# A hybrid decoder layer on one core: TensorE's order from the output projection on, the first feed-forward block's partial sums and the norm's row sums rearranged

## The chip, the core and the metric

The kernel runs on one core of a Trainium2 chip. The metric is the device time of one execution in microseconds (us). A core has five engines with an instruction stream each: TensorE (PE; its weight loads are shown apart, as PEld), VectorE (DVE), ScalarE (ACT), GpSimd (POOL) and SyncE (SP, which here only issues transfers). Each works through its own stream in order; they wait for each other by semaphores. Matmul results are collected in PSUM banks, which VectorE and ScalarE read.

## What is computed

One layer with batch 1, 512 tokens, width 1024, in float32. Two attention branches run side by side, are gated and merged, and a SwiGLU feed-forward part follows:

```python
u = rms_norm(x, norm_mix_g)
proj = u @ w_in
...
merged = sigmoid(gate_sb) * y_sb + sigmoid(gate_dl) * y_dl
x = x + merged @ w_out
u2 = rms_norm(x, norm_ffn_g)
g_ff, up_ff = split(u2 @ w_ffn_in, 2)          # each 512 x 2816
x = x + (silu(g_ff) * up_ff) @ w_ffn_out
return rms_norm(x, norm_final_g)

def rms_norm(x, g):
    return x * rsqrt(mean(x * x, -1) + 1e-6) * g
```

## The kernel before, in words

**Layout.** Everything is kept feature-major: 128 features on the partitions, 512 tokens along the row, so that x is eight tiles of 128x512. Weights stand still in TensorE, activations move through it. Every float32 product is made of three matmuls in fp32r, on numbers split into a high part (a cast) and a low part (what the cast left over): high·high, high·low, low·high. For weights, ScalarE makes the high part (`whi`, L147) and VectorE the low part (`wlo`, L148). `next_weights()` hands out the next chunk of weights and splits two chunks ahead; the raw chunks are loaded by SyncE into a few rotating buffers.

**Stages.** Norm and input projection, the two attentions, the up-projections with their gates (they leave the merged activations as eight pairs mh, ml: the high and low parts of the eight feature tiles), the output projection, the feed-forward part, the last norm.

**Output projection** (before: from L770). It makes its eight feature tiles f in the order of HALVES = 0, 4, 1, 5, 2, 6, 3, 7. Each is 24 matmuls of 128x512 (8 values of k, three each) into a bank `po`; there are two such banks, so the third projection takes over the first one's. VectorE adds the bank to x (`res`, L774). Then come the operands of the feed-forward part: `forms_upper` for f < 4, `forms_lower` for f >= 4, which needs the matching upper one, and ScalarE squares x for the norm, which VectorE sums up in `acc`.

**Feed-forward block 0, 1, 2, ...** (`hidden(i)`). The kernel does the 22 blocks of the first feed-forward product with seven products in place of eight, in the manner of Strassen and Winograd. The seven operands are called B11, U1, B21, B22, T3, V2, T4. They are the seven quarters of 256 columns of `fh` (high parts) and `fl` (low parts), one such tile for each of four values of k; the last three (T3, V2, T4) are computed from both halves of x (`forml`, L763 to L765), cast on ScalarE (`fh`, L174) and their low part is made on VectorE (`fl`, L175, 128x768). The last value of k, 3, is ready last, as it needs the last projection f = 7. Of weights a block has four chunks: unit 0 (for B11 and B21), unit 1 (V2 and T3), unit 2 (U1 and T4) and unit 3 (B22). Units 1 and 2 share one load, `rawu`: VectorE adds its two loaded thirds into a third one (L136), unit 2 is split from it, and unit 1 from its sum with unit 0's raw chunk (`s`, L138). There are two buffers of rawu: that of block 2 can be loaded when block 0's unit 2 has been split into whi and wlo.

The sums are collected in two PSUM banks, `pf` (halves pa and p6) and `pg` (halves psum and pr). `times(ps, unit, half, form, ks)` issues three 128x256 matmuls for each k (L816, L817, L818 before the change). Some sums must be read in between: ScalarE copies q1, yv (from pa), q7 (from pr) and wv (L824). In block 0 the norm's factors are not known yet, so block 0 is finished later and the norm is put on the results.

**Norm.** `row_sums()` issues four small matmuls (L283, `ss`) on acc; VectorE scales the sums (L287), GpSimd raises them to the power -1/2 (`r`, L291). `row_spread()` spreads r over the partitions (`rb`, L298), in block 1, ahead of which nothing needs it.

**Order.** Each engine's order is chosen by a scheduler from the order of the program, with priorities (`tc.high_priority()`). Within `tc.manual_schedule(engines={PE})` TensorE's order is that of the program. Before, that began at the feed-forward loop (L966); the order of the other engines is the scheduler's throughout.

Of the kernel before, what the change touches and what calls it, by code (L numbers as in the profile page):

```python
# [16 lines left out]
P = 128  # L17
S = 512
D = 1024
KD = D // P  # L20
# [9 lines left out]
HALVES = [0, 4, 1, 5, 2, 6, 3, 7]  # L30
# [14 lines left out]
def trunk_kernel(ctx, tc, xT, gains, w_in, w_up, w_o, w_f, w_d, bias, out):  # L45
# [20 lines left out]
    def bank(tag, name):  # L66
        if tag == "proj":
            return pp.tile([P, S], F32, tag=tag, name=name, bufs=BANKS[tag])
        if ppool[1] is not None:
            return ppool[1].tile([P, S], F32, tag="att" if tag == "alpha" else "sums", name=name, bufs=BANKS["att"])  # L70
        return pair(name)[:, 0, :]
# [286 lines left out]
    def next_weights(ahead=2):  # L358
        w = weights(ci[0], ahead)
        ci[0] += 1  # L360
        return w

    def product(ps, mh_, ml_, w, nk, first=True, last=True, k0=0, between={}):
        hi, lo = w
        for k in range(nk):
            cs = slice(k * P, (k + 1) * P)
            mm3(ps, hi[:, cs], lo[:, cs], mh_[k0 + k], ml_[k0 + k], first and k == 0, last and k == nk - 1)
            tick()
            if k in between:
                with tc.high_priority():  # L370
                    between[k]()
# [385 lines left out]
    def forms_lower(j):  # L757
# [8 lines left out]
        V.scalar_tensor_tensor(out=lo[:, 2:4, :], in0=halves(x), scalar=g, in1=hi[:, 2:4, :].bitcast(F32), op0=ALU.mult, op1=ALU.subtract)  # L766
        split_to(hi[:, 4:, :], lo[:, 4:, :], raw)

    for f in HALVES:
        x = res(f)  # L770
        ps = bank("proj", f"po{f}")
        product(ps, mhi, mlo, next_weights(), KD)
        with tc.high_priority():
            V.tensor_tensor(out=x, in0=ps, in1=x, op=ALU.add)  # L774
        with tc.high_priority():
            if f >= 4:
                forms_lower(f - 4)
            else:
                forms_upper(f)
        norm_square(f, x, acc2, "2")  # L780

    def row_sums():
        ps = bank("att", "ss2")
        for j in range(4):
            row_sum(ps, acc2, j)
        rows["r2"] = row_factors(ps, 4, "2")
# [16 lines left out]
    def hidden(i):  # L803
# [7 lines left out]
        def times(ps, unit, half, form, ks=range(4), first=False, last=False):  # L811
            hi, lo = w[unit]
            for k in ks:
                cs = slice(half * S + k * P, half * S + (k + 1) * P)
                xhi, xlo = fh[k][:, form, :], fl[k][:, form, :]
                T.matmul(ps, hi[:, cs], xhi, start=first and k == 0, stop=False, skip_group_check=True)  # L816
                T.matmul(ps, hi[:, cs], xlo, start=False, stop=False, skip_group_check=True)  # L817
                T.matmul(ps, lo[:, cs], xhi, start=False, stop=last and k == 3, skip_group_check=True)  # L818

        def kept(ps, name):  # L820

            t = lsq[:, :hs] if name == "q1" and i == 0 else fp.tile([P, hs], F32, tag=f"kept{name}", name=f"{name}{i}")
            with tc.high_priority():
                A.copy(t, ps)  # L824
            return t
# [6 lines left out]
        if i == 0:  # L832

            w[1] = next_weights()
            times(pa, 0, 0, B11, first=True)
            q1 = kept(pa, "q1")
            times(psum, 0, 1, B21, range(3), first=True)
            w[2] = next_weights()
            times(pa, 2, 0, U1)
            yv = kept(pa, "yv")  # L840
            times(pr, 1, 1, T3, range(3))
            times(p6, 1, 0, V2, range(3))
            times(psum, 0, 1, B21, [3], last=True)
            times(pr, 1, 1, T3, [3])
            q7 = kept(pr, "q7")
            times(p6, 1, 0, V2, [3])
            wv = kept(p6, "wv")
            V.tensor_tensor(out=yv, in0=yv, in1=wv, op=ALU.add)
            w[3] = next_weights()
            times(pr, 2, 1, T4, last=True)  # L850
            times(pa, 3, 0, B22, last=True)
            V.tensor_tensor(out=g[:, hs:], in0=pa, in1=wv, op=ALU.add)
            V.tensor_tensor(out=wv, in0=wv, in1=q1, op=ALU.add)
        else:
            times(pa, 0, 0, B11, first=True)
            q1 = kept(pa, "q1")
            times(psum, 0, 1, B21, first=True, last=True)
            w[1] = next_weights()
            times(pa, 1, 0, V2)
            wv = kept(pa, "wv")  # L860
            times(pr, 1, 1, T3)
            q7 = kept(pr, "q7")
            if i == 1:
                row_sums()
            if i == 4:
                row_inverse()
            w[2] = next_weights()
            times(pa, 2, 0, U1)
            yv = kept(pa, "yv")
            times(pr, 2, 1, T4, last=True)  # L870
            if i == 1:
                row_spread()
                yield
            w[3] = next_weights()
            times(pa, 3, 0, B22, last=True)
# [87 lines left out]
            T.matmul(pw, warm, warm.unsqueeze(1).to_broadcast([P, 4, P]), start=True, stop=True)  # L963

    waiting = []
    order = tc.manual_schedule(engines={mybir.EngineType.PE})  # L966
    order.__enter__()
    for step in FFN:
        if step[0] == "in":
            waiting.append(hidden(step[1]))  # L970
# [100 lines left out]
```

## Time and profile before

| | us |
|---|---|
| median of 3 runs | 750.01 (749.42 to 750.14) |
| the profiled execution | 750.42 |
| its span (first to last instruction) | 748.7 |
| TensorE busy | 739.3 (99%) |
| VectorE busy | 530.0 (71%) |
| ScalarE busy | 365.8 (49%) |
| GpSimd busy | 80.4 (11%) |

The profile shows one execution. The mean granted TensorE clock is 0.997 of full speed. Rows below give start and duration in us, then engine, line, operation and tiles (out<-in); a bracket gives the time that the engine stood idle before the instruction, and what ended it.

### The profile page before, as it was taken

What the parts mean: (1) busy time and instruction counts of PE and PEld (TensorE: products, weight loads), DVE (VectorE), ACT (ScalarE), POOL (GpSimd) and SP (SyncE); (2) the same over time, 40 slices, a digit from 0 to 9 for tenths busy, and PEclk for the clock granted to TensorE, in tenths of its full rate; (3) what the DMA queues carried; (4) which work ended last, traced back from release to release, by engine and by line L of the source; (5) the groups of instructions that cost most, each with busy time, mean ns of one, the idle gap of its engine ahead of it and who ended that gap; (6) DMA issues with size and microseconds to landing.
All of it is one profiled execution on the core that took longest, in us unless ns stands there. A gap on an engine that the chain in (4) does not pass through costs nothing. (4 is left out here: it accounts for less than half of the span.)

```text
span 748.7 us, 10944 instructions
## 1 busy us (share of the span) xinstructions
PE 739.3 (99%) x4447; PEld 644.6 (86%) x4447; DVE 530.0 (71%) x685; ACT 365.8 (49%) x526; POOL 80.4 (11%) x48
## 2 busy tenths in 40 slices
PE   9999999999999999999999999999999999999996
PEld 6877777889888888888889999999999999999985
DVE  6446676576768883376997899778787777776643
ACT  7255756752423632332654666545445454444453
POOL 1005042250241030000001000000000000000033
PEclk9999999999999999999999999999999999999998
DMA  8322112122342232234313223233332333332223
GB/s 281 113 61 96 69 57 85 57 85 84 114 167 78 94 113 77 78 115 153 113 56 99 100 78 114 92 105 105 108 109 84 104 106 108 104 104 66 57 57 114
DMA packets 25187, 74.13 MB, mean 99 GB/s; under 512 B 2864, under 2 KB 5936, under 8 KB 25008
## 3 DMA queue, kind: packets, MB, share of 16 engines
q1 hardware_dynamic: 23664, 69.74, 28.8%
q0 software_dynamic: 784, 3.15, 1.2%
q8 instruction: 35, 0.57, 0.3%
q10 hardware_dynamic: 688, 0.54, 0.2%
q14 instruction: 16, 0.13, 0.1%
HBM read 71.32 MB, written 2.10 MB: 98 GB/s over the span
## 5 line engine op out<-in xcount | busy, mean ns | idle before, releaser
L147 ACT CAST whi<-raw 128x1024 fp32r<-128x1024 f32 (+2 forms) x114 | 108.7, 955 | 146.1 <-PE pg L817 33.9
L148 DVE TENSOR_TENSOR wlo<-raw,whi 128x1024 fp32r<-128x1024 f32 (+2 forms) x114 | 145.9, 1281 | 40.9 <-ACT whi L147 39.9
L816 PE MATMUL pf<-fh,whi 128*128 128x256 f32 x348 | 98.7, 284 | 0.1
L818 PE MATMUL pf<-fh,wlo 128*128 128x256 f32 x348 | 98.6, 283 | 0.0
L817 PE MATMUL pf<-fl,whi 128*128 128x256 f32 x348 | 98.5, 283 | 0.0
L816 PE MATMUL pg<-fh,whi 128*128 128x256 f32 x264 | 75.2, 285 | 0.6 <-ACT q L824 0.6
L817 PE MATMUL pg<-fl,whi 128*128 128x256 f32 x264 | 74.7, 283 | 0.0
L818 PE MATMUL pg<-fh,wlo 128*128 128x256 f32 x264 | 74.7, 283 | 0.0
L816 PEld LDWEIGHTS pf<-fh,whi 128*128 128x128 f32 x348 | 66.7, 192 | 0.9 <-ACT lsq L824 0.3
L817 PEld LDWEIGHTS pf<-fl,whi 128*128 128x128 f32 x348 | 66.7, 192 | 0.6
L818 PEld LDWEIGHTS pf<-fh,wlo 128*128 128x128 f32 x348 | 66.7, 192 | 0.3 <-DVE wlo L148 0.2
L147 ACT CAST whi<-s 128x1024 fp32r<-128x1024 f32 (+1 forms) x43 | 36.2, 842 | 33.8 <-PE pg L817 21.5
L148 DVE TENSOR_TENSOR wlo<-s,whi 128x1024 fp32r<-128x1024 f32 (+1 forms) x43 | 41.2, 959 | 14.9 <-ACT whi L147 14.7
L816 PEld LDWEIGHTS pg<-fh,whi 128*128 128x128 f32 x264 | 50.6, 192 | 1.3 <-ACT q L824 1.0
L817 PEld LDWEIGHTS pg<-fl,whi 128*128 128x128 f32 x264 | 50.6, 192 | 0.0
L818 PEld LDWEIGHTS pg<-fh,wlo 128*128 128x128 f32 x264 | 50.6, 192 | 0.0
L163 PE MATMUL pd<-hh,whi 128*128 128x512 f32 (+1 forms) x132 | 50.4, 382 | 0.0
L163 PE MATMUL pd<-hl,whi 128*128 128x512 f32 (+1 forms) x132 | 50.3, 381 | 0.0
L163 PE MATMUL pd<-hh,wlo 128*128 128x512 f32 (+1 forms) x132 | 50.1, 379 | 0.0
L920 POOL TENSOR_TENSOR inv<-inv,sq 128x256 f32<-128x256 f32 (+1 forms) x10 | 9.6, 963 | 317.4 <-ACT sq L919 315.3
L914 DVE TENSOR_TENSOR res<-pd,res 128x512 f32<-128x512 f32 (+1 forms) x36 | 22.6, 629 | 20.9 <-PE pd L163 20.7
L147 ACT CAST whi<-rawu 128x1024 fp32r<-128x1024 f32 x22 | 23.1, 1051 | 29.0 <-PE pd L163 23.5
(464 smaller groups left out, 1788.2 us busy)
## 6 DMA issues: line engine op xcount, KB each, us to landing
raw<-in_w_in_dram SPq DMA_DIRECT2D x43, 512.0 KB, 3.3
rawu<-in_w_ffn_in_dram SPq DMA_DIRECT2D x22, 512.0 KB, 3.2
raw<-in_w_ffn_in_dram SPq DMA_DIRECT2D x22, 512.0 KB, 3.4
raw<-in_w_ffn_out_dram SPq DMA_DIRECT2D x24, 384.0 KB, 3.1
raw<-in_w_out_dram SPq DMA_DIRECT2D x8, 512.0 KB, 3.3
raw<-in_w_up_dram SPq DMA_DIRECT2D x8, 384.0 KB, 3.0
x<-in_xT_dram SPq DMA_DIRECT2D x8, 256.0 KB, 4.2
res<-in_xT_dram POOLq DMA_DIRECT2D x8, 256.0 KB, 4.2
```

The source lines that it names most:

```text
L147: state["last"] = A.copy(hi[:, cs], r[:, cs])
L148: V.tensor_tensor(out=lo[:, cs], in0=r[:, cs], in1=hi[:, cs].bitcast(F32), op=ALU.subtract)
L163: return T.matmul(ps, a, b, start=start, stop=stop, skip_group_check=not check)
L816: T.matmul(ps, hi[:, cs], xhi, start=first and k == 0, stop=False, skip_group_check=True)
L817: T.matmul(ps, hi[:, cs], xlo, start=False, stop=False, skip_group_check=True)
L818: T.matmul(ps, lo[:, cs], xhi, start=False, stop=last and k == 3, skip_group_check=True)
L914: newest[1] = V.tensor_tensor(out=x, in0=ps, in1=x, op=ALU.add)
L920: G.tensor_tensor(out=rows["inv"][:, cs], in0=rows["inv"][:, cs], in1=sq[:, cs], op=ALU.add)
```

## The change

The output projection is issued by a new `out_part(f, ks)`, which can issue some values of k alone. TensorE's order is fixed by the program from there on: seven of the eight k of f=0, two of f=4, the last of f=0, the rest of f=4, and then one projection after the other. In block 0 the first three k of T3 and V2 are issued ahead of U1, and at its end the last k of T3 (with the copy q7) ahead of that of B21. The row sums are called at the end of block 0 instead of in block 1. Lines of the blocks move down by 15: L774 becomes L789, L816 to L818 become L831 to L833, L824 becomes L839.

```diff
--- before.py
+++ after.py
@@ -766,10 +766,25 @@
         V.scalar_tensor_tensor(out=lo[:, 2:4, :], in0=halves(x), scalar=g, in1=hi[:, 2:4, :].bitcast(F32), op0=ALU.mult, op1=ALU.subtract)
         split_to(hi[:, 4:, :], lo[:, 4:, :], raw)
 
+
+    begun = {}
+
+    def out_part(f, ks):
+        if f not in begun:
+            begun[f] = bank("proj", f"po{f}"), next_weights()
+        ps, (whi, wlo) = begun[f]
+        for k in ks:
+            cs = slice(k * P, (k + 1) * P)
+            mm3(ps, whi[:, cs], wlo[:, cs], mhi[k], mlo[k], k == 0, k == KD - 1)
+
+    order = tc.manual_schedule(engines={mybir.EngineType.PE})
+    order.__enter__()
+    out_part(HALVES[0], range(KD - 1))
+    out_part(HALVES[1], range(2))
     for f in HALVES:
         x = res(f)
-        ps = bank("proj", f"po{f}")
-        product(ps, mhi, mlo, next_weights(), KD)
+        out_part(f, [KD - 1] if f == HALVES[0] else range(2 if f == HALVES[1] else 0, KD))
+        ps = begun[f][0]
         with tc.high_priority():
             V.tensor_tensor(out=x, in0=ps, in1=x, op=ALU.add)
         with tc.high_priority():
@@ -835,20 +850,21 @@
             times(pa, 0, 0, B11, first=True)
             q1 = kept(pa, "q1")
             times(psum, 0, 1, B21, range(3), first=True)
+            times(pr, 1, 1, T3, range(3))
+            times(p6, 1, 0, V2, range(3))
             w[2] = next_weights()
             times(pa, 2, 0, U1)
             yv = kept(pa, "yv")
-            times(pr, 1, 1, T3, range(3))
-            times(p6, 1, 0, V2, range(3))
-            times(psum, 0, 1, B21, [3], last=True)
             times(pr, 1, 1, T3, [3])
             q7 = kept(pr, "q7")
+            times(psum, 0, 1, B21, [3], last=True)
             times(p6, 1, 0, V2, [3])
             wv = kept(p6, "wv")
             V.tensor_tensor(out=yv, in0=yv, in1=wv, op=ALU.add)
             w[3] = next_weights()
             times(pr, 2, 1, T4, last=True)
             times(pa, 3, 0, B22, last=True)
+            row_sums()
             V.tensor_tensor(out=g[:, hs:], in0=pa, in1=wv, op=ALU.add)
             V.tensor_tensor(out=wv, in0=wv, in1=q1, op=ALU.add)
         else:
@@ -860,8 +876,6 @@
             wv = kept(pa, "wv")
             times(pr, 1, 1, T3)
             q7 = kept(pr, "q7")
-            if i == 1:
-                row_sums()
             if i == 4:
                 row_inverse()
             w[2] = next_weights()
@@ -963,8 +977,6 @@
             T.matmul(pw, warm, warm.unsqueeze(1).to_broadcast([P, 4, P]), start=True, stop=True)
 
     waiting = []
-    order = tc.manual_schedule(engines={mybir.EngineType.PE})
-    order.__enter__()
     for step in FFN:
         if step[0] == "in":
             waiting.append(hidden(step[1]))
```

TensorE, at the end of the first two projections, before (po0 and po4 are the banks of f=0 and f=4, po1 that of the third projection, f=1; mh7 and ml7 are the last pair of merged activations):

```order
L163 MATMUL po4_2704<-mh5_2579,wlo55_2620 128x512
L163 MATMUL po0_2664<-mh7_2647,whi54_2585 128x512
L163 MATMUL po4_2704<-mh6_2613,whi55_2619 128x512
L163 MATMUL po4_2704<-ml6_2614,whi55_2619 128x512
L163 MATMUL po4_2704<-mh6_2613,wlo55_2620 128x512
L163 MATMUL po0_2664<-ml7_2648,whi54_2585 128x512
L163 MATMUL po0_2664<-mh7_2647,wlo54_2586 128x512
L163 MATMUL po4_2704<-mh7_2647,whi55_2619 128x512
L163 MATMUL po4_2704<-ml7_2648,whi55_2619 128x512
L163 MATMUL po4_2704<-mh7_2647,wlo55_2620 128x512
L163 MATMUL po1_2747<-mh0_2409,whi56_2667 128x512
L163 MATMUL po1_2747<-ml0_2410,whi56_2667 128x512
```

After the change, at the end of f=0:

```order
L163 MATMUL po4_2694<-mh1_2443,whi55_2619 128x512
L163 MATMUL po4_2694<-ml1_2444,whi55_2619 128x512
L163 MATMUL po4_2694<-mh1_2443,wlo55_2620 128x512
L163 MATMUL po0_2666<-mh7_2647,whi54_2585 128x512
L163 MATMUL po0_2666<-ml7_2648,whi54_2585 128x512
L163 MATMUL po0_2666<-mh7_2647,wlo54_2586 128x512
L163 MATMUL po4_2694<-mh2_2477,whi55_2619 128x512
L163 MATMUL po4_2694<-ml2_2478,whi55_2619 128x512
L163 MATMUL po4_2694<-mh2_2477,wlo55_2620 128x512
```

The last part of f=0 has moved from among the last matmuls of f=4 to ahead of f=4's third k; 18 matmuls of f=4 now stand between it and the third projection, which begins at the same place as before.

TensorE, at the last k of block 0's sums (whi62, whi63 and whi64 are the weights of units 0, 1 and 2: with pg, whi63 is T3, whi62 is B21 and whi64 is T4; with pf, whi63 is V2), before:

```order
L816 MATMUL pg0_3009<-fh3_2950,whi62_2920 128x256
L817 MATMUL pg0_3009<-fl3_2951,whi62_2920 128x256
L818 MATMUL pg0_3009<-fh3_2950,wlo62_2921 128x256
L816 MATMUL pg0_3009<-fh3_2950,whi63_2962 128x256
L817 MATMUL pg0_3009<-fl3_2951,whi63_2962 128x256
L818 MATMUL pg0_3009<-fh3_2950,wlo63_2963 128x256
L816 MATMUL pf0_3008<-fh3_2950,whi63_2962 128x256
L817 MATMUL pf0_3008<-fl3_2951,whi63_2962 128x256
L818 MATMUL pf0_3008<-fh3_2950,wlo63_2963 128x256
L816 MATMUL pg0_3009<-fh0_2697,whi64_3012 128x256
```

After:

```order
L831 MATMUL pg0_3009<-fh3_2952,whi63_2964 128x256
L832 MATMUL pg0_3009<-fl3_2953,whi63_2964 128x256
L833 MATMUL pg0_3009<-fh3_2952,wlo63_2965 128x256
L831 MATMUL pg0_3009<-fh3_2952,whi62_2922 128x256
L832 MATMUL pg0_3009<-fl3_2953,whi62_2922 128x256
L833 MATMUL pg0_3009<-fh3_2952,wlo62_2923 128x256
L831 MATMUL pf0_3008<-fh3_2952,whi63_2964 128x256
L832 MATMUL pf0_3008<-fl3_2953,whi63_2964 128x256
L833 MATMUL pf0_3008<-fh3_2952,wlo63_2965 128x256
L831 MATMUL pg0_3009<-fh0_2712,whi64_3012 128x256
```

The last k of T3 and of B21 have changed places; V2's and T4's are where they were. Ahead of these rows U1 (12 matmuls) now stands behind T3's and V2's first 18 and not ahead of them, and the two first matmuls of B11 that stood ahead of the last projection now stand behind it. The row sums follow B22's 12 matmuls, which come behind T4's.

VectorE, behind the last projection (res3 and po7 belong to f=7; wlo64 is the low half of block 0's unit 2, rawu71 the raw chunk of block 2), before:

```order
L774 TENSOR_TENSOR res3_2370<-po7_2959,res3_2370 128x512
L763 SCALAR_TENSOR_TENSOR forml3_2994<-res3_2370,gt_70,form3_2949 128x256
L764 SCALAR_TENSOR_TENSOR forml3_2994<-res3_2370,ng_2662,form3_2949 128x256
L148 TENSOR_TENSOR wlo64_3013<-rawu63_2875,whi64_3012 128x1024
L766 SCALAR_TENSOR_TENSOR fl3_2951<-res3_2370,gt_70,fh3_2950 128x512
L765 SCALAR_TENSOR_TENSOR forml3_2994<-res3_2370,ng_2662,forml3_2994 128x256
L194 TENSOR_TENSOR acc2_2660<-acc2_2660,sq2_7_3002 128x512
L175 TENSOR_TENSOR fl3_2951<-forml3_2994,fh3_2950 128x768
L136 TENSOR_TENSOR rawu71_3095<-rawu71_3095 128x512
L138 TENSOR_TENSOR s2371_3261<-rawu71_3095,raw70_3043 128x1024
```

After:

```order
L789 TENSOR_TENSOR res3_2370<-po7_2961,res3_2370 128x512
L148 TENSOR_TENSOR wlo64_3013<-rawu63_2877,whi64_3012 128x1024
L763 SCALAR_TENSOR_TENSOR forml3_2996<-res3_2370,gt_70,form3_2951 128x256
L764 SCALAR_TENSOR_TENSOR forml3_2996<-res3_2370,ng_2662,form3_2951 128x256
L766 SCALAR_TENSOR_TENSOR fl3_2953<-res3_2370,gt_70,fh3_2952 128x512
L194 TENSOR_TENSOR acc2_2660<-acc2_2660,sq2_7_3004 128x512
L765 SCALAR_TENSOR_TENSOR forml3_2996<-res3_2370,ng_2662,forml3_2996 128x256
L136 TENSOR_TENSOR rawu71_3095<-rawu71_3095 128x512
L175 TENSOR_TENSOR fl3_2953<-forml3_2996,fh3_2952 128x768
L138 TENSOR_TENSOR s2371_3261<-rawu71_3095,raw70_3061 128x1024
```

fl3 from forml3 and the sum of rawu71 (L136) have changed places, and wlo64, made from rawu63, has moved two places ahead. On ScalarE the copy q7 has moved ahead of the cast whi66, so that the copy wv now follows the casts whi66 and whi67, where before only whi67 stood between the two copies.

## Rows read from the trace of the kernel before

**Rows 1.** Page, part 1: busy us (share of the span) x instructions.
```profile
PE 739.3 (99%) x4447; PEld 644.6 (86%) x4447; DVE 530.0 (71%) x685; ACT 365.8 (49%) x526; POOL 80.4 (11%) x48
```

**Rows 2.** Waits of TensorE: us in total, times, longest us.
```profile
PE po L163 <- DVE res L774: 0.9, 1, 0.9
PE rb L298 <- POOL r L291: 0.6, 1, 0.6
PE pg L816 <- ACT q L824: 0.6, 1, 0.6
```

**Rows 3.** TensorE's timeline, around the third projection's start: start, us, line, operation.
```profile
355.02 0.39 PE L163 MATMUL po<-mh,wlo 128*128 128x512 f32 x1
356.26 0.50 PE L163 MATMUL po<-mh,whi 128*128 128x512 f32 x1 [0.86 <-DVE res L774]
...
360.03 0.39 PE L163 MATMUL po<-ml,whi 128*128 128x512 f32 x1
```

**Rows 4.** VectorE's timeline, the last low half of the merged activations.
```profile
348.50 0.69 DVE L175 TENSOR_TENSOR ml<-gs,mh 128x512 fp32r<-128x512 f32 x1 [0.69 <-ACT mh L174]
```

**Rows 5.** TensorE's timeline, from the last projection through block 0's last parts.
```profile
389.08 0.39 PE L163 MATMUL po<-mh,wlo 128*128 128x512 f32 x1
...
391.46 0.28 PE L818 MATMUL pg<-fh,wlo 128*128 128x256 f32 x1
...
392.53 0.28 PE L816 MATMUL pf<-fh,whi 128*128 128x256 f32 x1
...
396.72 0.28 PE L818 MATMUL pf<-fh,wlo 128*128 128x256 f32 x1
397.57 0.39 PE L816 MATMUL pg<-fh,whi 128*128 128x256 f32 x1 [0.57 <-ACT q L824]
```

**Rows 6.** TensorE's timeline in block 1: row sums and spread.
```profile
406.31 0.95 PE L283 MATMUL ss<-ones,acc 128*128 128x1 f32 x8
...
409.96 0.28 PE L818 MATMUL pg<-fh,wlo 128*128 128x256 f32 x1
410.84 1.16 PE L298 MATMUL rb<-ident,r 128*128 128x128 f32 x8 [0.60 <-POOL r L291]
```

**Rows 7.** VectorE's timeline behind the last projection.
```profile
391.03 1.22 DVE L148 TENSOR_TENSOR wlo<-rawu,whi 128x1024 fp32r<-128x1024 f32 x1
...
394.20 0.96 DVE L175 TENSOR_TENSOR fl<-forml,fh 128x768 fp32r<-128x768 f32 x1 [0.30 <-ACT fh L174]
396.95 0.69 DVE L136 TENSOR_TENSOR rawu<-rawu 128x512 f32<-128x512 f32 x1 [1.79 <-DMA rawu<-in_w_ffn_in_dram]
```

**Rows 8.** ScalarE's timeline behind the last projection.
```profile
389.28 1.06 ACT L147 CAST whi<-rawu 128x1024 fp32r<-128x1024 f32 x1 [1.46 <-PE po L163]
...
396.20 1.05 ACT L147 CAST whi<-raw 128x1024 fp32r<-128x1024 f32 x1 [1.75 <-PE pg L817]
397.15 0.37 ACT L824 COPY q<-pg 128x256 f32<-128x256 f32 x1
```

**Rows 9.** rawu's transfer: SyncE's issue; DMA view 392 to 397; its 22 landings.
```profile
392.27 0.33 SPq L111 DMA_DIRECT2D rawu<-in_w_ffn_in_dram  x1
...
q8 instruction: 1, 0.02, 1.1%
...
rawu<-in_w_ffn_in_dram SPq DMA_DIRECT2D x1, 512.0 KB, 4.7
...
DMA to landing us min/median/max: 3.1/3.2/5.2
```

**Rows 10.** TensorE at start and end; windows 744 to 745 (0.66 is the clock).
```profile
6.57 0.61 PE L163 MATMUL first<-xl,whi 128*128 128x512 f32 x1
7.00 0.41 PE L163 MATMUL first<-xh,whi 128*128 128x512 f32 x1
...
741.45 1.16 PE L298 MATMUL rb<-ident,r 128*128 128x128 f32 x8 [0.15 <-POOL r L937]
...
744.00:745.00 1.00, 0.00 (x0) 0.00 (x0) 0.08 (x1) 0.00 (x0) 0.36 (x1) 0.66 1.04 335
```

## The prediction

> **What bounds the kernel now.** I read the page first: TensorE is busy in 99% of the span [rows 1], so nothing that only another engine does can show in the time, and a change of order can win no more than the microseconds in which TensorE stands still. Then the waits of TensorE, longest first [rows 2]: in the body there are three of note, for the add behind the first output projection, for the root r, and for the copy q7. Then TensorE's timeline around each of them, because the waits view counts only the idle part: after a stop the first matmul lasts 0.50 where its neighbours last 0.39, or 0.39 where they last 0.28 [rows 3, 5], so a stop costs 0.11 us more than its bracket. Undisturbed, a 512-wide step of the projection takes 0.229 us (16 steps from 356.26 to 360.03, less that 0.11 [rows 3]), a 256-wide step of the feed-forward block 0.12 (35 steps from 392.53 to 396.72 [rows 5]). Last the timelines of VectorE and ScalarE at the same place, to see what each copy and each low half waits behind. I write T for the start of the last matmul of the output projection, 389.08 [rows 5].
>
> **What goes.** Four stops lie on TensorE's path, so all of each counts.
> 1. The third projection takes over the bank of the first. Before, the first one's end was mixed into the second one's end. 17 steps from 355.02 to 360.03 took 5.01 us and not 3.89 [rows 3]: 1.12. Now 18 matmuls of the second projection, 4.1 us, stand between the last of f=0 and the third one, and f=0's add stands right behind the low half ml7 on VectorE. Nothing new is late: the moved last part of f=0 is needed 20 steps ahead of 355.02, at 350.4, and ml7 is done at 349.19 [rows 4].
> 2. U1 came right behind B21's first nine matmuls, ahead of both the copy q1 (its bank) and the low half wlo of its weights: 391.46 to 392.53 is 1.07 for four steps, so 0.59 over 0.48 [rows 5]. Now 18 matmuls of T3 and V2 stand between and cover it.
> 3. The stop for q7: 396.72 to 397.57 is 0.85 for one step of 0.12, plus 0.11 of restart: 0.84 [rows 5]. q7 stood behind the cast whi on ScalarE (396.20, 1.05 long [rows 8]).
> 4. The stop at rb for r: 409.96 to 410.84, 0.88 for a step of 0.12: 0.76 [rows 6]. The row sums now stand at the end of block 0, 48 matmuls earlier, and r is there long before rb. The row sums themselves (0.95 us for their eight records [rows 6]) cost the same at either place, and their VectorE and GpSimd steps lie beside matmuls.
>
> Together 3.31 us. The two matmuls of the feed-forward block that the scheduler had put ahead of the last projection now follow it: the same work, nothing.
>
> **What comes.** Three waits that the trace of before doesn't have, at most in another place.
> 5. The largest: T3's last part now needs fl3, the low half of the last four forms, and on VectorE that now stands *behind* the sum of rawu (L136), which waits for a transfer. Before, it stood ahead of it: fl at 394.20, then 1.79 us of waiting, then L136 at 396.95 [rows 7]. The transfer is issued when wlo has read the old buffer: whi runs from T+0.20 for 1.06 [rows 8], wlo then to T+2.52 (0.04 later, an estimate like the hand-overs of item 6, and 1.22 long [rows 7]), the issue follows 0.02 us after, as 392.27 follows 391.03+1.22 [rows 7, 9]: T+2.54. With L for the time from issue to landing, L136 (0.69) and fl (0.96) [rows 7] and 0.03 between put T3's second matmul at T+4.22+L. TensorE would be there after 51 matmuls (12 of B11, 9 of B21, 9 of T3, 9 of V2, 12 of U1) and one more: T+0.23+52×0.12 = T+6.47. L of such a transfer is 3.1 at the least, 3.2 in the middle and 5.2 at the most; the one at this very place took 4.7, with a fetch of instructions (q8) in its window [rows 9]. So even the shortest makes TensorE wait, 0.85 us, the longest 2.95. I take 4.2, midway between the usual one and the longest, since the fetch comes back at the same place of TensorE's program but not at the same distance from the issue: 1.95 us of waiting and 0.11 of restart, 2.06.
> 6. B21's last part writes to the same bank as T3, and now stands right behind it, so it waits for the copy q7 with nothing between: last matmul 0.28, hand-over 0.05, copy 0.37 [rows 8], hand-over 0.05 (397.15+0.37 to 397.57), 0.75 in place of a step of 0.12, and 0.11 of restart: 0.74. Its bounds are 0 and the 0.84 of item 3, the nearest row; I take the worked value, since q7 no longer stands behind a cast.
> 7. wv stands on ScalarE now behind two casts instead of one, and B22 writes to its bank. Let S be the start of B21's last part. Before, S was 396.72 less 8 steps, 395.76, and the first cast began at S+0.44 [rows 5, 8]; with the restart now S+0.55. Casts follow each other at 0.95 (396.20 to 397.15 [rows 8]), so wv begins at S+2.45 and B22 can start at S+2.87. TensorE gets there after 18 matmuls and the restart, at S+2.27: 0.60, and 0.11: 0.71. Its bounds: 0 (the second cast done in the shadow) and 0.95 more (another cast in front).
>
> Together 3.51 us. Later blocks gain and lose nothing that I can find: their order is untouched, and their weights come as before.
>
> **Sum.** 3.51 − 3.31 = 0.20 us slower, in general L − 4.0. Against the profiled execution (750.42, span 748.7) that is 750.62; the median of the runs is 0.41 lower, so **750.2**. A measurement of this kernel can tell about 0.2%, 1.5 us, from no change: faster begins at 748.5, slower at 751.5. Four stops go, and three of the same total take their place.
>
> **Rivals.**
> *No fetch in the way* (16%). The instruction fetch is no hindrance, and the transfer lands in the usual 3.2 us: L − 4.0 is −0.8, **749.2**. For it speaks that 3.2 is the middle of the 22 transfers; against it that the one at this place took 4.7 with a fetch inside [rows 9]. The Trainium skill (Runtime: NRT & Kernel Launch, Instruction fetch mechanics) says that each engine streams its program in blocks over a DMA queue of its own while it runs, at a cost that is "mostly hidden". By that rule the fetch adds nothing to a neighbouring transfer and 749.2 would be the sum; the trace's 4.7 against its usual 3.2 disagrees as far as one transfer can.
> *The four stops go and nothing, or little, comes* (16%). If VectorE passes fl3 before the transfer matters, and the two copies are hidden, the time is 750.0 − 3.3 = **746.7**; with items 6 and 7 alone, 1.45, it is 748.1. It asks for a landing of 2.25 us or less after the issue (4.22+L ≤ 6.47), or for an issue a microsecond earlier than I put it; the shortest landing on record is 3.1 [rows 9], and the order on VectorE is plain in the rows shown above. That the reorder does not take place at all is excluded by the same rows. I still give it a sixth, since my three new waits are all inferred.
> *The clock falls in the new wait* (10%), the other side. The longest stop of TensorE in the body was 0.9 us [rows 2] and its steps went on at full rate; the new one is 1.95. At the kernel's end, the last matmul ends at 742.61, and the mean granted clock of 744 to 745 is 0.66 [rows 10], a mix of 1.00 and 0.50 (2.4 and 1.2 GHz) that puts the fall at about 744.3: 1.7 us of idleness were enough there, though TensorE had been working thinly before them and is dense before mine. [...] The price: the one stretch of half-rate steps in this trace is at the start, 0.43 from 6.57 to 7.00 against 0.229 later [rows 3, 10], and it ends there, so at most 7.0 us at half rate, 3.5 lost: 750.2 + 3.5 = **753.7**. The Trainium skill (TensorE: Matmul & The Clock Gate, Why this matters for your kernels) warns of idle gaps between bursts of matmuls for this reason; no stop in the body of this trace shows it.
>
> **Chances and range.** The forecast itself, with L from 3.6 to 5.2 (749.6 to 751.2), has 58%. It, the first rival (749.1 to 749.5) and the upper end of the second (to 748.0, some 6%) make the range 748.0 to 751.2, with about 80%. Faster by over 0.2%: the second rival, 16%. Slower: the third, 10%. Between them 74%.
>
> **What would show it.** In TensorE's waits of the changed kernel the three entries of before are gone, and in their place stand about 2 us for fl (VectorE L175) at T3's last part, 0.6 for q7 ahead of B21's last part, and 0.5 for wv ahead of B22. On VectorE L136 stands ahead of fl, with an idle time that ends with the transfer of rawu at 6 to 7 us after T; its landing is 3.6 to 5.2. From the last matmul of f=0 to the third projection TensorE runs without a gap. I am wrong if the wait for fl is missing or under 0.8 us, if TensorE's steps behind it are 0.24 apart, or if a wait stands in block 1 or later that before did not have.

## The result, and the profile after

| | before | changed |
|---|---|---|
| median | 749.55 us (748.74 to 750.36, 21 runs) | 750.5 us (749.78 to 752.23, 21 runs) |
| ratio | | 1.0014, 95% interval 1.0008 to 1.0020 |
| the profiled execution | 750.42, span 748.7 | 751.67, span 750.0 |

The change makes no difference of more than 0.2%, as forecast; it costs 0.95 us, where 0.2 were forecast, and the range (748.0 to 751.2) holds it. The profiled execution of before, from which the forecast was worked out, is 0.87 us above the median of these 21 runs; the experiments come back to that.

The page: TensorE is as full as before [rows 1].

```profile
span 750.0 us, 10945 instructions
PE 740.0 (99%) x4447; PEld 645.5 (86%) x4447; DVE 530.1 (71%) x685; ACT 365.8 (49%) x526; POOL 79.5 (11%) x48
```

TensorE's waits in the changed kernel, against [rows 2]: the entries for the projection's add and for r (L291) are gone, that for q7 has stayed under its new line, and one for fl is new and the longest.

```profile
PE pg L832 <- DVE fl L175: 1.9, 1, 1.9
...
PE pg L831 <- ACT q L839: 0.5, 1, 0.5
```

TensorE's timeline from the last matmul of the output projection to the spread of r, against [rows 3, 5, 6]. T is now 387.88.

```profile
387.88 0.39 PE L163 MATMUL po<-mh,wlo 128*128 128x512 f32 x1
...
394.22 0.28 PE L831 MATMUL pg<-fh,whi 128*128 128x256 f32 x1
396.42 0.38 PE L832 MATMUL pg<-fl,whi 128*128 128x256 f32 x1 [1.92 <-DVE fl L175]
396.64 0.28 PE L833 MATMUL pg<-fh,wlo 128*128 128x256 f32 x1
397.38 0.39 PE L831 MATMUL pg<-fh,whi 128*128 128x256 f32 x1 [0.46 <-ACT q L839]
...
397.84 0.30 PE L831 MATMUL pf<-fh,whi 128*128 128x256 f32 x1
397.95 0.40 PE L832 MATMUL pf<-fl,whi 128*128 128x256 f32 x1
398.15 0.41 PE L833 MATMUL pf<-fh,wlo 128*128 128x256 f32 x1
...
400.93 0.41 PE L831 MATMUL pf<-fh,w 128*128 128x256 f32 x1
...
401.35 0.29 PE L833 MATMUL pf<-fh,w 128*128 128x256 f32 x1
...
402.57 0.95 PE L283 MATMUL ss<-ones,acc 128*128 128x1 f32 x8
...
412.25 1.05 PE L298 MATMUL rb<-ident,r 128*128 128x128 f32 x8
```

T3's last part begins at 394.22 and its second matmul stands until 396.42; B21's last part stands for q7 until 397.38. From 397.95 on a step takes 0.21 us in place of 0.12, up to 401.35. Before the ss rows nothing waits for wv (B22 begins at 400.93 at the slow pace), and rb waits for nothing. The clock over the same stretch, by windows (the third number from the right is the granted clock, 1.00 for 2.4 GHz, 0.50 for 1.2 GHz):

```profile
396.00:398.00 2.00, 1.12 (x7) 0.91 (x8) 1.50 (x2) 0.45 (x2) 0.00 (x0) 0.99 0.00 0
398.00:400.00 2.00, 2.00 (x11) 2.00 (x11) 1.00 (x1) 2.00 (x3) 0.00 (x0) 0.50 0.00 0
400.00:402.00 2.00, 2.00 (x14) 2.00 (x13) 1.06 (x3) 1.19 (x2) 0.00 (x0) 0.66 0.34 102
402.00:404.00 2.00, 2.00 (x20) 2.00 (x19) 2.00 (x3) 0.05 (x1) 0.00 (x0) 1.00 0.41 160
```

VectorE's timeline at the same place, against [rows 7]: L136 has waited 1.96 us for its transfer, and fl stands right behind it.

```profile
389.17 1.23 DVE L148 TENSOR_TENSOR wlo<-rawu,whi 128x1024 fp32r<-128x1024 f32 x1 [0.17 <-ACT whi L147]
...
394.80 0.69 DVE L136 TENSOR_TENSOR rawu<-rawu 128x512 f32<-128x512 f32 x1 [1.96 <-DMA rawu<-in_w_ffn_in_dram]
395.41 0.95 DVE L175 TENSOR_TENSOR fl<-forml,fh 128x768 fp32r<-128x768 f32 x1
```

The transfer, against [rows 9], is issued right behind wlo, in SyncE's timeline:

```profile
390.42 0.33 SPq L111 DMA_DIRECT2D rawu<-in_w_ffn_in_dram  x1
```

and lands 4.4 us later, as the DMA view from its issue to its landing has it (tile, KB, us to landing):

```profile
rawu<-in_w_ffn_in_dram SPq DMA_DIRECT2D x1, 512.0 KB, 4.4
```

So in this pair of profiles the losses are 2.18 for fl (396.42 − 394.22, less a step of 0.12, plus 0.10 of restart), 0.73 for q7 (397.38 − 396.64, less 0.12, plus 0.11) and 1.47 for the slow clock (17 steps from 397.84 to 401.35 in 3.51 us, where 0.12 each make 2.04), 4.38 together. Against the 3.31 of the four stops of before that is +1.07. The spans differ by 1.3; another 0.23 lies ahead of the output projection, whose first matmul starts at 344.59 and not at 344.36.

### The profile page after: what moved, and what is told of

The parts are those of the page before. It is cut to its first block, busy times and chain, and to the rows that moved or that the text cites. A ratio compares the mean times of both kernels' runs of the same rounds, so it can differ in the third digit from the quotient of the medians.

```text
span 750.0 us, 10945 instructions
## 1 busy us (share of the span) xinstructions
PE 740.0 (99%) x4447; PEld 645.5 (86%) x4447; DVE 530.1 (71%) x685; ACT 365.8 (49%) x526; POOL 79.5 (11%) x48
## 4 chain that ended last, share of the span: by engine, by line
PE 97%; DMA 1%; DVE 0%; issue 0%; ACT 0%; POOLq 0%; SPq 0%; POOL 0%
PE pd L163 16%; PE pjgd L163 6%; PE pjgs L163 6%; PE po L163 6%; PE pf L831 5%; PE pf L832 5%; PE pf L833 5%; PE pvvd L163 5%; PE pjdk L163 4%; PE pjdq L163 4%; PE up L163 4%; PE pg L831 4%; PE pg L832 4%; PE pg L833 4%; PE pvvs L163 3%; PE pjsq L163 2%
## 5 line engine op out<-in xcount | busy, mean ns | idle before, releaser
L831 PE MATMUL pf<-fh,whi 128*128 128x256 f32 x348 | 98.7, 283 | 0.0
L833 PE MATMUL pf<-fh,wlo 128*128 128x256 f32 x348 | 98.6, 283 | 0.0
L831 PE MATMUL pg<-fh,whi 128*128 128x256 f32 x264 | 75.8, 287 | 0.5 <-ACT q L839 0.5
L833 PE MATMUL pg<-fh,wlo 128*128 128x256 f32 x264 | 75.2, 285 | 0.0
L831 PEld LDWEIGHTS pf<-fh,whi 128*128 128x128 f32 x348 | 66.7, 192 | 0.6
L833 PEld LDWEIGHTS pf<-fh,wlo 128*128 128x128 f32 x348 | 66.9, 192 | 0.0
L831 PEld LDWEIGHTS pg<-fh,whi 128*128 128x128 f32 x264 | 51.2, 194 | 1.2 <-ACT q L839 0.8
L833 PEld LDWEIGHTS pg<-fh,wlo 128*128 128x128 f32 x264 | 51.2, 194 | 0.0
```

## The experiments

The theory was that fl, behind a transfer on VectorE, is the loss, and that q7 and wv add their copies. The rivals: that block 0's new order brings the wait, whatever VectorE does; that the clock does it; that the stops of before are not what one profile shows.

### fl ahead of the sum of rawu

```diff
-        split_to(hi[:, 4:, :], lo[:, 4:, :], raw)
+        state["fl"] = split_to(hi[:, 4:, :], lo[:, 4:, :], raw)
...
-            V.tensor_tensor(out=u[:, 0, :], in0=u[:, 1, :], in1=u[:, 2, :], op=ALU.add)
+            us = V.tensor_tensor(out=u[:, 0, :], in0=u[:, 1, :], in1=u[:, 2, :], op=ALU.add)
+            if i == 71:
+                tc.add_manual_dep(us.ins, state["fl"].ins.name, NOSYNC, reason="issue order")
```

> The changed kernel, with one thing undone: on VectorE the low half fl of the last forms stands again ahead of the sum of rawu (L136), which waits for its transfer. Theory (the order on VectorE is the loss): the wait of 1.9 us at T3's last part shrinks to the 0.4 that the chain of forms itself is late (fl would start at 393.72, when ScalarE's cast ends, and end at 394.67, against 394.34), the steps behind it stay at 0.12 us, and in place of the half-rate steps a wait for wv of about 0.5 shows ahead of B22. Gains of 3.3 less 0.5, 0.7 and 0.7: about 748.1, 1.4 under the kernel before, 2.3 under the changed one. Rival (it is block 0's new order that asks for T3's last part too early, whatever VectorE does): a wait of 1.5 us or more stays there, and the time stays within 0.5 us of the changed kernel's 750.5.

Measured: 749.28 us (11 runs), 0.9992 of before (0.9983 to 1.0001). TensorE's waits in the body:

```profile
PE pg L833 <- ACT q L841: 0.5, 1, 0.5
PE pf L833 <- ACT wv L841: 0.4, 1, 0.4
...
PE pg L834 <- DVE fl L177: 0.3, 1, 0.3
```

The waits are those of the theory, one by one: fl 0.3, q7 0.5, wv 0.4, no slow steps. The rival falls: block 0's order alone does not make the long wait. But the time is 1.2 us above the 748.1 that the theory gave. As all that the sum says of this kernel is there, the error is to be looked for on the other side, in the kernel before.

### Each part of the change alone

Only the order from the output projection on (block 0 and the row sums as before):

```diff
-            times(pr, 1, 1, T3, range(3))
-            times(p6, 1, 0, V2, range(3))
             w[2] = next_weights()
             times(pa, 2, 0, U1)
             yv = kept(pa, "yv")
+            times(pr, 1, 1, T3, range(3))
+            times(p6, 1, 0, V2, range(3))
+            times(psum, 0, 1, B21, [3], last=True)
             times(pr, 1, 1, T3, [3])
             q7 = kept(pr, "q7")
-            times(psum, 0, 1, B21, [3], last=True)
...
-            row_sums()
...
+            if i == 1:
+                row_sums()
```

> The kernel before with the fixed order from the output projection on, alone: block 0's order and the place of the row sums are as before. In its built order VectorE has fl behind the sum of rawu, as in the changed kernel. Theory (this part of the change brings the wait for the transfer): the stop of 0.9 for the first projection's add is gone (1.1 us gained), the stops at U1, for q7 and at rb stay, and a wait for fl of about 1.2 us stands at T3's last part, as U1 stands ahead of it and takes 0.6 of it: about 749.7, no change to the kernel before. Rival (block 0's order brings the wait): no wait for fl, 1.1 us under the kernel before, 748.4.

Measured: 749.69 us, 0.9999 (0.9985 to 1.0013), with the widest spread of all, 748.41 to 753.17 in 11 runs; the profiled execution is one of the longer ones (751.18). VectorE's timeline in it:

```profile
395.15 0.69 DVE L136 TENSOR_TENSOR rawu<-rawu 128x512 f32<-128x512 f32 x1 [2.07 <-DMA rawu<-in_w_ffn_in_dram]
395.75 0.95 DVE L175 TENSOR_TENSOR fl<-forml,fh 128x768 fp32r<-128x768 f32 x1
```

fl stands behind L136, as the theory has it, and TensorE's longest wait is for it:

```profile
PE pg L832 <- DVE fl L175: 1.6, 1, 1.6
```

The granted clock, by windows, falls here too, behind that wait, which ends at 396.76:

```profile
398.00:400.00 2.00, 2.00 (x13) 2.00 (x13) 2.00 (x2) 0.96 (x3) 0.00 (x0) 0.62 0.08 10
400.00:402.00 2.00, 2.00 (x12) 2.00 (x11) 1.77 (x4) 0.98 (x1) 0.00 (x0) 0.52 0.76 252
```

That the median is the theory's 749.7 is luck, as it does not come about by the theory's sum. The three stops that were to stay have gone or shrunk: in this profile U1 begins without a stop (a step of 0.12 us), T4 begins 0.27 us late, where q7 had cost 0.73 over a step before, and rb waits for nothing. The slow steps come instead.

Block 0's order alone is the same piece of the diff the other way round, in the kernel before:

> The kernel before with block 0's new order alone. In its built order VectorE has fl ahead of the sum of rawu. Theory: the stops at U1 (0.6) and for q7 behind the cast (0.8) go, a wait of 0.6 for q7 ahead of B21's last part and one of 0.6 for wv ahead of B22 come, and the wait for fl is under 0.3 us; the bank stop (0.9) and the rb stop (0.6) stay: no change, 749.5, and no fall of the clock. Rival (block 0's order brings the long wait): a wait for fl of about 2 us, and 751.5 or more.

Measured: 749.12 us, 0.9992 (0.9983 to 1.0001). On VectorE fl stands ahead of L136:

```profile
393.61 0.96 DVE L175 TENSOR_TENSOR fl<-forml,fh 128x768 fp32r<-128x768 f32 x1 [0.30 <-ACT fh L174]
394.87 0.69 DVE L136 TENSOR_TENSOR rawu<-rawu 128x512 f32<-128x512 f32 x1 [0.30 <-DMA rawu<-in_w_ffn_in_dram]
```

TensorE waits for the two copies, and hardly for the bank:

```profile
PE pg L816 <- ACT q L824: 0.5, 1, 0.5
PE pf L816 <- ACT wv L824: 0.4, 1, 0.4
PE po L163 <- DVE res L774: 0.2, 1, 0.2
```

The pair settles whose wait it is. It comes with TensorE's fixed order at the projection, since the scheduler then also orders VectorE anew, and not with block 0. What was not expected: in this kernel the bank stop, whose order is that of before, is 0.2 and not 0.9, and the stop at rb is missing, with the row sums where they were.

The row sums alone:

```diff
             times(pa, 3, 0, B22, last=True)
+            row_sums()
...
-            if i == 1:
-                row_sums()
```

> The kernel before with the row sums alone moved to the end of block 0. Theory (the rb stop is a race that a part of the executions loses): no rb stop, the other stops as before, 0 to 0.7 us gained, in the median about 0.3: 749.3, no difference that can be measured. Rival (the stop is in every execution): 0.8 gained, 748.8.

Measured: 749.3 us, 0.9995 (0.9987 to 1.0004): 0.4 in the medians, as the theory has it, but the interval holds no change and the rival's 0.8 as well. Against the rival speaks the kernel with block 0's order alone, which has its row sums where they were and no stop at rb.

### The two kernels profiled again

The kernel before, unchanged:

> The kernel before once more, unchanged, for a second profile of it. Theory (two of its four stops are races with a transfer of rawu, as VectorE has the projection's add and the scaled row sums behind a sum of rawu, and the profiled execution lost both): the stops at U1 and for q7 are there again with 0.6 and 0.8 us, but the bank stop (0.9) and the rb stop (0.6) are of another size, one of them under 0.4, and the span is nearer to 748.0 than to 748.7. Rival (the stops belong to the order and are the same in every execution): all four within 0.15 us of the first profile's.

Measured: 749.2 us, span 747.5. TensorE's waits:

```profile
PE pg L816 <- ACT q L824: 0.6, 1, 0.6
PE rb L298 <- POOL r L291: 0.3, 1, 0.3
...
PE po L163 <- DVE res L774: 0.2, 1, 0.2
```

Its timeline at the third projection, against [rows 3]:

```profile
354.81 0.39 PE L163 MATMUL po<-mh,wlo 128*128 128x512 f32 x1
355.38 0.50 PE L163 MATMUL po<-mh,whi 128*128 128x512 f32 x1 [0.17 <-DVE res L774]
```

The q7 stop is the same 0.6 (and that at U1 the same 0.59), as both follow from the order. The two others have shrunk, by the same formula as in the forecast: the bank stop to 0.57 − 0.23 + 0.11 = 0.45 (354.81 to 355.38, less a step, plus the restart), and rb to 0.48 (0.60 from the matmul ahead of it, less 0.12). Together the four are 2.35, not 3.31. Why they vary is in VectorE's order. The projection's add stands behind two sums of rawu, which wait for two transfers. In the first profile:

```profile
354.92 0.69 DVE L136 TENSOR_TENSOR rawu<-rawu 128x512 f32<-128x512 f32 x1 [0.59 <-DMA rawu<-in_w_ffn_in_dram]
355.53 1.28 DVE L774 TENSOR_TENSOR res<-po,res 128x512 f32<-128x512 f32 x2
```

In the second:

```profile
354.03 0.69 DVE L136 TENSOR_TENSOR rawu<-rawu 128x512 f32<-128x512 f32 x1 [0.47 <-DMA rawu<-in_w_ffn_in_dram]
354.64 1.29 DVE L774 TENSOR_TENSOR res<-po,res 128x512 f32<-128x512 f32 x2
```

The two transfers landed 4.2 and 5.2 us after their issue in the first profile, 3.6 and 4.5 in the second; what made the first ones late, the trace does not show. At rb, r follows the scaled row sums (L287), which VectorE reaches only behind a sum of rawu that waited 1.07 and 1.09 us for its transfer. With 2.35 in place of 3.31, the first experiment fits too: its three waits cost 0.51, 0.73 and 0.70, a gain of 0.41, where its median was 0.59 under that of the kernel before measured with it.

The changed kernel, unchanged:

> The changed kernel once more, unchanged. Theory (the wait at T3's last part is T+4.1 us plus the landing of rawu, and the clock falls behind it only where the wait is long): the wait for fl follows the landing one for one (landing 3.2: 0.8 of waiting; 4.4: 1.9; 4.9: 2.4), the q7 wait is 0.5 again, and if the landing is under 4 the clock stays at 1.00 and a wait for wv of 0.4 shows, the span then being 748.1 to 748.8. Rival (the wait has another source): a wait of 1.9 whatever the landing.

Measured: 751.57 us, span 749.9, with a wait of 1.2 us for its first operands at the very start, 0.5 in the other profiles at most. TensorE's waits:

```profile
PE pg L832 <- DVE fl L175: 1.6, 1, 1.6
...
PE pg L831 <- ACT q L839: 0.5, 1, 0.5
PE pf L831 <- ACT wv L839: 0.4, 1, 0.4
```

rawu's landing, in the DMA view:

```profile
rawu<-in_w_ffn_in_dram SPq DMA_DIRECT2D x1, 512.0 KB, 4.1
```

The wait for fl follows the landing: 1.92 with 4.4, 1.64 with 4.1. The clock stays at 1.00 here, and the wait for wv shows, with 0.44. The losses are 1.90 (1.92 from matmul to matmul, less a step, plus 0.10 of restart), 0.73 and 0.70 by the same formula, 3.33 in all. Against the 2.35 of before's second profile that is 0.98 slower, against 0.95 in the medians; so close a match of two single executions is partly chance. Their spans differ by 2.4: 1.06 of it lies ahead of the output projection (the wait at the start) and 0.3 behind block 1, neither of which the change touches.

### The clock

The changed kernel with matmuls on zeros in TensorE's wait, eight (1.55 us of TensorE's time in the profile) and four (0.68 us, not the 0.9 expected):

```diff
             yv = kept(pa, "yv")
+            keep_clock(8)
             times(pr, 1, 1, T3, [3])
```

> The changed kernel with eight matmuls on zeros (128x512, bf16, into a spare bank) put on TensorE between U1 and T3's last part, where it waits for fl. They change no result, and no engine's order but TensorE's. Theory (the clock falls because of the idle wait, in some executions): T3's last part starts where it did, about 8.5 us after T, the granted clock stays at 1.00 behind it with steps of 0.12 us, and a wait for wv of 0.5 us shows ahead of B22. The runs' median is about 750.2 with a narrower spread, none over 751.2. Rival 1 (the fall has nothing to do with this wait): clock and spread are as in the changed kernel, 749.8 to 752.2. Rival 2 (the extra matmuls delay what follows): 751.5 or more.

> The changed kernel with four matmuls on zeros, 0.9 us, in the wait for fl: as much as the wait is at the shortest landing of 3.2, so that they delay no execution. Theory (the idle wait lets the clock fall in a part of the executions, and shorter idleness does not): the waits are as in the changed kernel less 0.9, the clock stays at 1.00 behind them, and the median is 750.1 with no run over 751.2. Rival (the fall comes whatever TensorE does in the wait, or needs less idleness than 1 us): half-rate steps behind T3's last part, or runs up to 752 as in the changed kernel.

Measured: with eight 750.66 us (750.33 to 751.35), with four 750.41 us (749.83 to 751.73, two of 11 runs over 751.2). TensorE with eight, then with four:

```profile
394.05 1.90 PE L978 MATMUL warm<-warm 128*128 128x512 bf16 x8
395.60 0.47 PE L831 MATMUL pg<-fh,whi 128*128 128x256 f32 x1
```

```profile
394.76 0.47 PE L831 MATMUL pg<-fh,whi 128*128 128x256 f32 x1
395.31 0.38 PE L832 MATMUL pg<-fl,whi 128*128 128x256 f32 x1
```

In both profiles the clock stays at 1.00, but in both the transfer landed early (3.2 and 3.4 us), so the wait would have been short anyway: the profiles are no evidence for the clock. Nor are the medians. Against the kernel before measured with them the two are at 1.0011 and 1.0010, the changed kernel at 1.0014, all within each other's intervals; and one of the 11 runs with eight and two of those with four are over 751.2, where the theory had none.

The mean granted clock of each single run says more. Half rate for 3.4 us lowers a run's mean by 0.002. The two profiled executions with a fall read 0.995 and 0.996, those without read 0.997 to 0.999, so a run at 0.997 may still hide a fall. At 0.996 or less are:

| version | runs at 0.996 or less |
|---|---|
| changed kernel | 7 of 21 |
| projection's order alone | 4 of 11 |
| changed, four filling matmuls | 1 of 11 |
| changed, eight filling matmuls | 0 of 11 |
| the six versions here with fl ahead of L136 | 0 of 61 |
| kernel before, measured with them | 0 of 76 |

So the fall belongs to the kernels with the long wait for fl, and it becomes rare when matmuls fill that wait; rival 1 of the eight falls by that, and rival 2 by the median of 750.66. It is not the main part of the loss: the 14 other runs of the changed kernel have a median of 750.3, 0.7 above the kernel before. In the profiles a fall was seen behind 1.92 and 1.62 us of waiting for fl, and none behind 1.64. What decides between them is open.

### Versions that keep the gains

First fl ahead of the sum of rawu as in the first experiment, the square's add behind the last form in the same manner, and block 0's last parts in another order (where the changed kernel's calls for U1 and V2's last part are taken out):

```diff
+            w[2] = next_weights(1)
+            times(pa, 2, 0, U1, range(3))
             times(pr, 1, 1, T3, [3])
             q7 = kept(pr, "q7")
+            times(pa, 2, 0, U1, [3])
+            yv = kept(pa, "yv")
+            times(p6, 1, 0, V2, [3])
+            wv = kept(p6, "wv")
             times(psum, 0, 1, B21, [3], last=True)
```

> A version that keeps the changed kernel's gains and takes its three new waits away by order alone: on VectorE fl stands ahead of the sum of rawu and the square's add behind the last form; in block 0 the order is three parts of U1, T3's last part, U1's last part, V2's last part, B21's last part, T4, B22 (so that six matmuls cover the copy q7 and 15 the copy wv). Theory: no wait of TensorE over 0.2 us from the third projection to block 2, the clock at 1.00 throughout, and 1.7 us under the first experiment of the fl order: about 747.5, 0.9973 of the kernel before. Rival (the waits hide others that then show): over 748.7.

Measured: 748.44 us, 0.9983 (0.9974 to 0.9992): better than both kernels, 0.9 short of the expectation. One wait had been overlooked: V2's last part writes to the bank that yv is being copied from.

```profile
PE pf L835 <- ACT yv L843: 0.5, 1, 0.5
```

So V2's last part goes ahead of U1's, and the copies behind both:

```diff
             q7 = kept(pr, "q7")
+            times(p6, 1, 0, V2, [3])
             times(pa, 2, 0, U1, [3])
             yv = kept(pa, "yv")
-            times(p6, 1, 0, V2, [3])
             wv = kept(p6, "wv")
...
-                A.copy(t, ps)
+                state["kept"] = A.copy(t, ps)
...
             state["last"] = A.copy(hi[:, cs], r[:, cs])
+            if i == 66:
+                tc.add_manual_dep(state["last"].ins, state["kept"].ins.name, NOSYNC, reason="issue order")
```

> The better version with the wait that it had left taken away: V2's last part comes ahead of U1's last part, and both copies yv and wv are made after both of them and ahead of the casts whi of block 1. Theory: the wait of 0.46 for yv (0.74 with its restart) goes, no other comes, as 15 matmuls cover the two copies; 747.8, 0.9974 of the kernel before. Rival (the two copies end after the 15 matmuls, or the low half of block 1's first weights now comes late behind the sum of rawu): a wait of 0.5 or more at B22 or at the start of block 1, and no gain on 748.4.

Measured: 747.55 us (747.33 to 747.81), **0.9968 of before (0.9955 to 0.9980)**. TensorE's waits in it, as the view lists them, but the warm-up's at the start; none stands between the output projection and the kernel's last rows, as the rb here is that of the final norm:

```profile
PE first L167 <- ACT xh L190: 0.5, 1, 0.5
PE first L167 <- DVE xl L191: 0.3, 1, 0.3
PE rb L304 <- POOL r L958: 0.2, 1, 0.2
```

What the list leaves out is 0.18 us for fl at T3's last part (393.96 to 394.26, less a step). That all four stops of before and the three new ones can go fits the ledger of the second profile: 749.69 − 2.35 is 747.3.

The smallest edit to the changed kernel that pays puts wlo of unit 2 behind the last form (`state["form"]` is the instruction at L765):

```diff
-            V.tensor_tensor(out=lo[:, cs], in0=r[:, cs], in1=hi[:, cs].bitcast(F32), op=ALU.subtract)
+            ls = V.tensor_tensor(out=lo[:, cs], in0=r[:, cs], in1=hi[:, cs].bitcast(F32), op=ALU.subtract)
+            if i == 64:
+                tc.add_manual_dep(ls.ins, state["form"].ins.name, NOSYNC, reason="issue order")
```

> The changed kernel with one thing moved: on VectorE the low half wlo of block 0's unit 2 stands behind the last form and not ahead of the first; by that the scheduler also puts fl ahead of the sum of rawu again. Theory: fl is done at about T+5.7, under the T+6.47 at which T3's last part asks for it, so that no wait is left there; the transfer of rawu starts 1.7 us later and still serves block 1 in time; the waits for q7 and wv stay: 0.4 to 0.5 under the first experiment's 749.3, so 748.8, 0.9987 of the kernel before. Rival (the later transfer now holds VectorE up and block 1's first weights come late): a wait for wlo at the start of block 1, 749.5 or more.

Measured: 748.61 us, 0.9986 (0.9977 to 0.9994). The wait for fl is gone, those for q7 and wv have stayed at 0.5 and 0.4, and block 1 waits for nothing.

## Why the prediction was right, and where its size was off

The direction and the mechanism held: four stops go, and three waits take their place. The two totals are further apart than forecast: 0.95 us in the medians and not 0.20. That the time itself, 750.2, lies within 0.3 of the measured 750.5 is partly luck: it was counted from a median of three runs (750.01) that is 0.46 above that of the 21 later ones, which hides more than half of the 0.75 that the difference was short of. Point by point:

| step of the forecast | forecast | first profiles | second profiles |
|---|---|---|---|
| 1 bank of the third projection | −1.12 | −1.12 | −0.45 |
| 2 U1 | −0.59 | −0.59 | −0.59 |
| 3 q7 | −0.84 | −0.84 | −0.83 |
| 4 rb | −0.76 | −0.76 | −0.48 |
| 5 fl behind the transfer | +2.06 | +2.18 | +1.90 |
| 6 q7 ahead of B21 | +0.74 | +0.73 | +0.73 |
| 7 wv ahead of B22 | +0.71 | 0 | +0.70 |
| the clock | – | +1.47 | 0 |
| sum | +0.20 | +1.07 | +0.98 |

**The terms that were mis-sized** are in the sum's first half: steps 1 and 4 were taken from one execution as if they belonged to the order ("four stops lie on TensorE's path, so all of each counts"). Both are races with transfers of rawu that VectorE waits for, and that execution lost both by more than the others seen. In the second profile they are 0.93 and not 1.88; with block 0's order alone the bank's stop is 0.43 and that at rb is gone, with the row sums alone the bank's is 0.59. (Step 4 also leaves out the restart that steps 1 to 3 add: from rb to the next matmul it is 0.91 us with the stop and 0.81 without. With that 0.10 the four are 3.41 and 2.45.) The forecast noticed that its profiled execution was 0.41 over the median and put that aside as an offset; it was the very thing to ask about, since the larger stops of that execution were what the change was credited with.

**Step 5** was right in place, cause and size. T3's second matmul follows the start of L136 by 1.6 us in three profiles (396.42 − 394.80 in the first), where the forecast's durations add up to 1.68; L was taken as 4.2 and was 4.4 and 4.1. What the forecast did not see is which part of the change brings it: the new order on VectorE comes from fixing TensorE's order at the projection, not from block 0, as the two parts alone show.

**Steps 6 and 7** were right to 0.01 us where no slow clock lay over them; in the first profile wv's wait was hidden, as the slow steps give the copy the time that it needs.

**The rivals.** That no fetch is in the way gave 749.2 with a landing of 3.2. The changed kernel's own two landings are 4.4 and 4.1, so it did not decide here; that landing does occur with the same order on VectorE (3.2 and 3.4 in the two kernels with filling matmuls). But a fetch does go with a late landing. Of the 260 transfers of rawu in the 13 profiles (without the two issued together in each), 211 have no start of a fetch (an entry q8 of the DMA view) from 0.3 us ahead of the issue to the landing, and 210 of these landed in 3.0 to 3.4 us, one in 3.9; the 26 with a fetch starting 0.1 to 2.4 us after the issue took 3.6 to 4.7. The other 23, with a fetch at the issue or later than that, took 3.1 to 4.9. No run moved a fetch on purpose, so that it causes the delay is not shown. In the changed kernel and the two with filling matmuls the fetch starts within 0.1 us ahead of the issue, and there 3.2, 3.4, 4.1 and 4.4 all occur; what decides between them is open. The rule of the Trainium skill (Runtime: NRT & Kernel Launch, Instruction fetch mechanics), "mostly hidden", is said of the fetch itself; that a neighbouring transfer pays nothing, as the forecast read it, does not agree with these landings. That little comes in place of the stops is refuted by the rows. That the clock falls in the new wait came true in the first profile, whose steps behind the wait are 0.21 us apart, close to the 0.24 that the forecast had named as a sign of being wrong; by the mean clocks it came true in at least 7 of the 21 runs, where the rival had 10%. It was mispriced: half rate lasted 3.4 us and cost 1.47, less the 0.70 of wv that it hid, and not 3.5. The Trainium skill (TensorE: Matmul & The Clock Gate, Why this matters for your kernels) warns of such gaps; this trace agrees with half the granted clock for 3.4 us behind 1.92 us of waiting.

## What to carry to other kernels

Before a stop is booked as a gain, ask what ends it: one that follows from the order is there in every execution, one that ends with a transfer is a race, and a single profile shows only one draw of it. When one engine's order is fixed by hand, look at the orders of the others in the built program, because a scheduler moves them too: here a low half slid behind an instruction that waits for a transfer, and TensorE's wait for it, 1.9 and 1.6 us in two profiles, took back most of what the change had gained. Moving one other low half on VectorE, by which it came ahead again, took the changed kernel from 1.0014 of the kernel before to 0.9986.

## What was not expected of the hardware

The granted clock halved within the body, behind a wait of 1.92 us in one execution and 1.62 in another, stayed at half for 3.4 us (397.95 to 401.35 in the first), and came back while TensorE went on working; behind 1.64 us in a third it did not fall. The same transfer of 512 KB landed 3.2, 3.4, 4.1, 4.4 and 4.5 us after its issue in the five executions that have this order on VectorE. The same 512 KB took 3.0 to 3.4 us in 210 of the 211 transfers of rawu that no fetch of instructions fell on, and 3.6 to 4.7 in all 26 where a fetch started 0.1 to 2.4 us after the issue.
